# Modulation rows loaded a step ahead, four subtractions moved to VectorE, and a later end for the last group

## The chip, the cores and the metric

The program runs on one core of a Trainium2 chip. Its time is the device time of one execution in microseconds (us). The core has a matrix engine (TensorE, PE in the profile), three engines for elementwise work (VectorE: DVE; ScalarE: ACT; GpSimd: POOL), and a queue on SyncE (SP) that issues nearly all the transfers between HBM and SBUF. Each engine, and the SP queue, takes its instructions strictly in program order; semaphores hold an instruction back until what it reads is there and what it overwrites has been read. Matrix products accumulate in PSUM, which is used as eight banks of 128x512 float32.

## What is computed

The reference is a stack of two layers on one sequence of 1024 tokens with 1024 features in float32. Layer 0 mixes tokens by a forgetting attention (16 heads), layer 1 by a gated linear attention (4 heads, chunks of 64). Each layer is followed by a SwiGLU network of 2816 hidden features. Every part takes an RMS norm that is scaled and shifted by a modulation computed from one conditioning vector, and its output is gated by it:

```python
    c_act = jax.nn.silu(c)
    for i in range(DEPTH):
        mod = c_act @ ada_w[i] + ada_b[i]
        sh1, sc1, g1, sh2, sc2, g2 = jnp.split(mod, N_MOD, axis=-1)
        h = modulate(rms_norm(x, norm1_g[i]), sh1, sc1)
        j = i // N_MIXERS
        if i % N_MIXERS == 0:
            y = forgetting_attention(h, fox_w_in[j], fox_b_f[j], fox_w_out[j])
        else:
            y = gated_linear_attention(h, gla_w_in[j], gla_w_a2[j], gla_b_a[j], gla_g_o[j], gla_w_out[j])
        x = x + g1[:, None, :] * y
        h = modulate(rms_norm(x, norm2_g[i]), sh2, sc2)
        x = x + g2[:, None, :] * swiglu(h, ffn_w_in[i], ffn_w_out[i])
    return rms_norm(x, final_g)
```

`modulate(h, shift, scale)` is `h * (1 + scale) + shift`. `ada_w` is 2 x 1024 x 6144, 48 MB, all of which is read: a modulation is a product of one vector with a 1024x1024 block for each layer and each of the six j.

## The kernel before

**Products.** Every matrix product is done in three passes (`mm3`, L237 to L239): both operands are split in a high and a low part (ACT makes the high part by a cast, L159, DVE the low part by a subtraction, L160), and high x high, low x high and high x low are summed in one PSUM bank. One pass is a matmul of 128x128 with 128x512. So each weight tile costs a load on SP, a cast on ACT, a subtraction on DVE and, where tiles are combined, additions on POOL (L672, L674, L684) before PE may use it.

**Stages.** FoX attention up to about 523 us of the profiled span, its output product and the first network FFN0 up to 1364, the GLA mixer and its output product up to 1817, the second network FFN1 up to the end. Both networks are the same function, `ffn`, on the two layers. It has five stretches:

1. the norm and the operands. Each matrix of h is cut in 2x2 blocks B11, B12, B21, B22 (features by tokens), and sums of blocks T1 to T4 are made as in Winograd's form of Strassen's product, which needs seven block products instead of eight. `second_half` (L1164) makes y12, y22 from x and the norm row, then the raw differences: T1 = y12-y11 on POOL (L1170), y12 = y22-y12 on POOL (L1172, T3 later), y22 = y22-y11 on DVE (L1173, T2), y21 = y21-y22 on POOL (L1176, T4 later). `split_t` splits each in a high part on ACT (L1132, L1135) and a low part on DVE (L1133, L1136).
2. plain tiles (`plain_tile`): a first pair of hidden tiles as ordinary products of 24 matmuls, 672 to 740 us in FFN0. In the trace their weights are called o_s and their banks p_b. At its end the T3 and T4 tiles are split, and `mid()` is called.
3. groups: hidden tiles in groups of seven products of 12 matmuls each (`prod`). ACT applies the Silu, DVE adds products (L1275, into views ex_s of slots "ex"), POOL multiplies gate and up half (L1261) and makes the hidden blocks' sums. 740 to 1100 us in FFN0.
4. output products in seven-product form, summed on DVE (L1447, L1449). In the last round the four groups i = 0..3 of two output rows each are put together: five additions on POOL (L1461 to L1465) and four gates on DVE (L1467, x + g2 * y).
5. the last chunk (`last_chunk`): eight ordinary tiles of 12 matmuls per half of the tokens, f0e01800p_b to f0e01870p_b (f1e... in FFN1), whose result DVE adds to x (L1029). Their banks are a ring pj of three.

**The modulation of layer 1.** The six vectors of layer 1 are computed beside other work. `ada_steps` (L336) is a generator; each step loads a 128-row piece of `ada_w` (L342, SP), multiplies it by a column of c_act (L346, L348, ACT), adds it to an accumulator (L349, POOL), and after eight steps PE sums over the partitions (L365, matmuls mp_b). `ada1` is a `Pace`: each product in the groups calls `ada1(0.64 * n)`, and the yields ADA_A and ADA_B are what a step costs in that currency. `mid0` queues j = 0 and 1 at FFN0's stretch 3 in pieces of 256 columns with an accumulator and **one** raw buffer, both in a view of "ex" (named ex_s); the mixer of layer 1 queues the other four in 512 columns with an accumulator and two raw buffers (named ad_s).

**What sets the order.** A list scheduler orders the whole program: it takes the instructions of the generators as written, models their durations and the semaphores, and puts each engine's instructions in the order in which its model could start them. The order on an engine is then fixed. In FFN0 it draws the modulation's steps ahead of where `mid0` stands: the first ones lie in the tail of the attention's output product, at 613.8 us.

The functions that the change touches, as they are before:

## Time and profile before

| what | us |
|---|---|
| median of 3 runs | 2495.55 |
| lowest, highest run | 2491.82, 2496.45 |
| profiled execution | 2496.43 |
| its span, first to last instruction | 2494.7 |
| PE busy in the span | 2405.8 (96%) |
| DVE, ACT, POOL busy | 1707.5, 1200.8, 1189.9 |

The profile is one execution with a time stamp for every instruction. The views used below are: the groups of instructions by line or by tile with their minimum, median and maximum duration in ns; the list of waits (an instruction, what released it, total us, times, longest); windows (a stretch of the span, the busy time of each engine in it with the count of instructions, the clock that TensorE was granted as a share of full speed, the share of time that DMA engines were busy, GB/s); and the timeline (start, duration, engine, line, instruction; in brackets the idle time ahead of it and what ended that). In the timeline instructions that follow one another on one line are put together in one row with their count and their time together. Names lose their buffer numbers: p_b is any bank of the networks' products, o_s any split weight tile.

### The profile page before, as it was taken

The page shows a single profiled execution, that of the slowest core. Times are in us where ns is not written, and L with a number is a line of the kernel's source. Part 1 is how long each engine was busy: PE and PEld are TensorE (multiplying, and loading weights), DVE is VectorE, ACT ScalarE, POOL GpSimd, SP SyncE. Part 2 cuts the span into 40 slices and gives each one's busy share as a digit, 9 for nine tenths or more (in the row PEclk, how much of TensorE's full clock was granted, in tenths as well). Part 3 has the DMA queues.
Part 4 walks back from the last instruction along what each step waited for, and adds up shares of the span by engine and source line. Part 5 has one row for each costly group of instructions (what it writes and reads, how often), then busy time and mean ns, then how long its engine had stood idle before and what let it go on. Part 6 is the DMA issues. An engine that isn't in the chain of part 4 may idle for free.

```text
span 2494.7 us, 35705 instructions
## 1 busy us (share of the span) xinstructions
PE 2405.8 (96%) x12458; PEld 2040.0 (82%) x12458; DVE 1707.5 (68%) x2829; ACT 1200.8 (48%) x2313; POOL 1189.9 (48%) x1060
## 2 busy tenths in 40 slices
PE   6999999999999989999999999999999999999998
PEld 5888888888878877778887888888878888888887
DVE  6577777676697666675788455445587667666787
ACT  4666565666444443444324665554344333345325
POOL 4233333332466766663354544443345666653263
PEclk9999999999999999999999999999999999999999
DMA  8223333232434544347664333325325434347653
GB/s 263 79 89 115 102 94 119 69 117 93 156 110 159 168 137 160 127 154 266 227 216 156 96 108 99 98 98 174 100 70 188 146 136 152 127 171 261 236 194 131
DMA packets 322813, 359.20 MB, mean 144 GB/s; under 512 B 18557, under 2 KB 255257, under 8 KB 322633
## 3 DMA queue, kind: packets, MB, share of 16 engines
q1 hardware_dynamic: 322632, 356.92, 42.8%
q8 instruction: 98, 1.61, 0.3%
q14 instruction: 83, 0.67, 0.1%
HBM read 268.19 MB, written 88.67 MB: 143 GB/s over the span
## 4 chain that ended last, share of the span: by engine, by line
PE 68%; DVE 10%; DMA 7%; POOL 6%; issue 4%; ACT 3%; SPq 1%; POOLq 0%; DVEq 0%; ACTq 0%
PE p_b L239 11%; PE p_b L237 11%; PE p_b L238 11%; DMA ex_s<-in_ada_w_dram 3%; PE t_b L922 2%; PE o_b L936 2%; PE qk_b L237 2%; PE qk_b L238 2%; PE qk_b L239 2%; DVE o_s L160 1%; DMA ad_s<-in_ada_w_dram 1%; DMA xv_s<-in_ffn_w_out_dram 1%; POOL ex_s L349 1%; PE s_b L891 1%; PE s_b L892 1%
## 5 line engine op out<-in xcount | busy, mean ns | idle before, releaser
L160 DVE TENSOR_TENSOR o_s<-xv_s,o_s 128x512 fp32r<-128x512 f32 (+1 forms) x376 | 328.7, 878 | 117.7 <-ACT o_s L159 117.2
L159 ACT CAST o_s<-xv_s 128x512 fp32r<-128x512 f32 (+1 forms) x376 | 216.2, 585 | 267.7 <-PE p_b L239 222.4
L237 PE MATMUL p_b<-B,o_s 128*128 128x512 f32 x608 | 239.8, 397 | 9.9 <-DVE ex_s L1275 8.1
L239 PE MATMUL p_b<-B,o_s 128*128 128x512 f32 x608 | 240.1, 396 | 8.2 <-DVE o_s L160 8.2
L238 PE MATMUL p_b<-B,o_s 128*128 128x512 f32 x608 | 239.8, 394 | 0.0
L902 POOL TENSOR_SCALAR lp_s<-lp_s,st 128x128 f32<-128x128 f32 (+7 forms) x128 | 95.9, 754 | 293.8 <-DVE st L901 260.7
L672 POOL TENSOR_TENSOR ex_s<-xv_s,xv_s 128x512 f32<-128x512 f32 (+1 forms) x64 | 86.8, 1357 | 254.7 <-DMA xv_s<-in_ffn_w_in_dram 90.7
L237 PE MATMUL p_b<-T,o_s 128*128 128x512 f32 x480 | 188.4, 393 | 6.0 <-ACT o_s L159 4.0
L238 PE MATMUL p_b<-T,o_s 128*128 128x512 f32 x480 | 186.9, 389 | 0.0
L239 PE MATMUL p_b<-T,o_s 128*128 128x512 f32 x480 | 183.5, 390 | 0.7 <-DVE o_s L160 0.7
L237 PEld LDWEIGHTS p_b<-B,o_s 128*128 128x128 f32 x608 | 116.0, 191 | 37.3 <-DVE ex_s L1275 9.8
L239 PEld LDWEIGHTS p_b<-B,o_s 128*128 128x128 f32 x608 | 116.0, 191 | 33.6 <-DVE o_s L160 9.0
L238 PEld LDWEIGHTS p_b<-B,o_s 128*128 128x128 f32 x608 | 116.1, 191 | 24.6 <-DVE B L1136 0.6
L900 ACT ACTIVATE lp_s<-lp_s,st 128x128 f32<-128x128 f32 (+7 forms) x128 | 99.3, 776 | 55.9 <-DVE st L896 55.3
L159 ACT CAST pt_s<-t_b 128x512 fp32r<-128x512 f32 (+1 forms) x160 | 80.1, 547 | 71.2 <-PE t_b L922 70.3
L1275 DVE TENSOR_TENSOR ex_s<-ex_s,p_b 128x512 f32<-128x512 f32 x140 | 93.5, 679 | 27.8 <-PE p_b L239 27.8
L237 PEld LDWEIGHTS p_b<-T,o_s 128*128 128x128 f32 x480 | 90.1, 188 | 27.4 <-ACT o_s L159 6.2
L160 DVE TENSOR_TENSOR pt_s<-t_b,pt_s 128x512 fp32r<-128x512 f32 (+1 forms) x160 | 96.5, 630 | 17.7 <-ACT pt_s L159 17.1
L239 PEld LDWEIGHTS p_b<-T,o_s 128*128 128x128 f32 x480 | 90.1, 188 | 21.4 <-DVE o_s L160 2.5
L238 PEld LDWEIGHTS p_b<-T,o_s 128*128 128x128 f32 x480 | 90.2, 188 | 18.3
L205 POOL TENSOR_TENSOR w_l_s<-w__s,w_h_s 128x256 fp32r<-128x256 f32 x90 | 69.6, 801 | 68.1 <-ACT w_h_s L202 58.6
L896 DVE CUSTOM_DVE_ANT_0 lp_s<-s_b,cum_s 128x512 f32<-128x512 f32 (+3 forms) x128 | 72.6, 569 | 40.5 <-PE t_b L922 22.9
(1941 smaller groups left out, 7636.2 us busy)
## 6 DMA issues: line engine op xcount, KB each, us to landing
xv_s<-in_ffn_w_in_dram SPq DMA_DIRECT2D x176, 256.0 KB, 3.0
hid_B<-x SPq DMA_DIRECT2D x70, 512.0 KB, 2.6
hid_T<-x SPq DMA_DIRECT2D x36, 512.0 KB, 2.7
xv_s<-in_ffn_w_out_dram SPq DMA_DIRECT2D x96, 192.0 KB, 4.4
ada_s<-in_ada_w_dram SPq DMA_DIRECT2D x32, 512.0 KB, 3.8
ad_s<-in_ada_w_dram SPq DMA_DIRECT2D x64, 256.0 KB, 2.7
xv_s<-in_ffn_w_out_dram SPq DMA_DIRECT2D x40, 256.0 KB, 3.0
T1o<-hid_T SPq DMA_DIRECT2D x18, 512.0 KB, 8.3
```

The lines of the kernel that those rows point to most:

```text
L159: nc.scalar.copy(hi, src)
L160: nc.vector.tensor_sub(lo, src, hi.bitcast(F32))
L205: (nc.gpsimd if i < 3 else nc.vector).tensor_sub(lo[:, cs], rw[:, cs], hi[:, cs].bitcast(F32))
L237: nc.tensor.matmul(ps, ah, bh, start=start, stop=False)
L238: nc.tensor.matmul(ps, ah, bl, start=False, stop=False)
L239: nc.tensor.matmul(ps, al, bh, start=False, stop=stop)
L672: nc.gpsimd.tensor_add(s1, a21, a22)
L896: nc.vector.tensor_tensor_reduce(lp[:, k0:k1], ps, cm[:, k0:k1], 1.0, mcur, ALU.add, ALU.min, mnew)
L900: nc.scalar.activation(lp, lp, AF.Exp, bias=mcur, scale=-1.0, accum_out=st[:, qi, 2:3])
L902: nc.gpsimd.tensor_scalar(lp, lp, st[:, qi, 3:4], 1.0, op0=ALU.mult, op1=ALU.mult)
L922: nc.tensor.transpose(tp[:, i, :], lps[qi][:, psl(2 * b + jj)], ident)
L1275: nc.vector.tensor_add(d, d if src is None else dest(G, src), ps)
```

## The change

Line numbers of the changed kernel are 11 to 30 higher: L342, L348, L349 become L345, L360, L361; L1029, L1461 to L1467 become L1040, L1478 to L1482.

1. **Modulation.** `ada_steps` issues the load of a step before it works on the step ahead of it (`got` holds one loaded piece in advance). In FFN0 the pieces have 512 columns instead of 256, and lie in views of slots "hid" with three raw buffers instead of one; these views are also ya, so they are free only when T2 and T4 are split. 64 loads of 128 KB become 32 of 256 KB, and the 64 multiplications and 56 additions become 32 and 28 of twice the width. The steps' costs are 6.0 and 3.0 instead of 5.0 and 2.5, and `ada1` is emptied before the group before the last, ahead of the tiles that take "hid" again.
2. **T3, T4.** The subtractions of T3 and T4 are done on DVE, and in the program they stand where T3 and T4 are split, behind the plain tiles. So that y22 and y12 last until then, T2's difference is written over y11 instead.
3. **Last group.** The five additions of the last group are done on DVE and are put, one or two at a time with the gates, behind the first outputs of the last chunk (`meanwhile`). The ring pj of the last chunk has six banks instead of three in layer 0 and four instead of three in layer 1.

```diff
--- before.py
+++ after.py
@@ -335,12 +335,24 @@
 
     def ada_steps(l, j, acc_of, raw_of, w):
 
+        steps = deque((c0, k) for c0 in range(0, D, w) for k in range(8))
+        got = deque()
+
+        def load():
+            if steps:
+                c0, k = steps.popleft()
+                raw = raw_of([P, w], F32, f"ada{l}{j}{c0}{k}")
+                nc.sync.dma_start(raw, ada_w[l, psl(k), j * D + c0:j * D + c0 + w])
+                got.append(raw)
+
         for c0 in range(0, D, w):
             acc = acc_of([P, w], F32, f"acc{l}{j}{c0}")
             for k in range(8):
-                raw = raw_of([P, w], F32, f"ada{l}{j}{c0}{k}")
-                nc.sync.dma_start(raw, ada_w[l, psl(k), j * D + c0:j * D + c0 + w])
+                if w == D or c0 == k == 0:
+                    load()
+                raw = got.popleft()
                 if w < D:
+                    load()
                     yield ADA_A
                     if k == 0:
                         nc.scalar.mul(acc, raw, cact[:, 0:1])
@@ -487,7 +499,6 @@
 
     sp_ins, rb_ins = [], []
     LATE1 = 7
-    TE = (nc.gpsimd, nc.gpsimd, nc.vector, nc.gpsimd)
     GK = (2, 6)
     SPM, RBM = (3, 4)
 
@@ -1031,7 +1042,7 @@
                 if after is not None:
                     after(m, hf)
 
-    def last_chunk(k0, kc, hs, xs, l, j, nm, v, norm, mt=2, each=None):
+    def last_chunk(k0, kc, hs, xs, l, j, nm, v, norm, mt=2, each=None, meanwhile=None):
 
 
         behind = None
@@ -1042,6 +1053,8 @@
                 sq(m, xs[m][:, hsl(h_)])
                 if each:
                     each(m, h_)
+                if meanwhile:
+                    meanwhile()
             run(out_chunk(k0, kc, hs, xs, l, j, f"{nm}{hf}", (hf,), after,
                           mt=mt, behind=behind))
             behind = norm(hf, sq.roots)
@@ -1167,13 +1180,10 @@
                 normed(y22[k], k + 4, 1, rb)
                 split_t(B22[k], y22[k], sh(k + 4))
             for k in range(4):
-                TE[0].tensor_sub(y11[k], y12[k], y11[k])
+                nc.gpsimd.tensor_sub(y11[k], y12[k], y11[k])
                 split_t(T1[k], y11[k])
-                TE[1].tensor_sub(y12[k], y22[k], y12[k])
-                TE[2].tensor_sub(y22[k], y22[k], y11[k])
-                split_t(T2[k], y22[k], sh(k + 4))
-            for k in range(4):
-                TE[3].tensor_sub(y21[k], y21[k], y22[k])
+                nc.vector.tensor_sub(y11[k], y22[k], y11[k])
+                split_t(T2[k], y11[k], sh(k + 4))
 
         x_sp = tc.dram_tile([8, P, S], F32, name=f"x_sp{l}")
         for k in range(8):
@@ -1312,10 +1322,12 @@
         block("T3", H_SL[4:8])
         T3 = b["T3"]
         for k in range(4):
+            nc.vector.tensor_sub(y12[k], y22[k], y12[k])
             split_t(T3[k], y12[k], ds[:, k:k + 1])
         block("T4", slots["to"])
         T4 = b["T4"]
         for k in range(4):
+            nc.vector.tensor_sub(y21[k], y21[k], y11[k])
             split_t(T4[k], y21[k])
         mid()
         bk = list(pin.q)
@@ -1361,7 +1373,7 @@
                     load_raw(ahead)
                 yield
 
-        hp, xr, zs = {}, {}, {}
+        hp, xr, zs, ends = {}, {}, {}, deque()
 
         def last_part():
 
@@ -1392,6 +1404,7 @@
         for X in gs[2:]:
             up = lambda n: advance(n) if X is gs[-1] else None
             if X is gs[-2]:
+                ada1.flush()
                 nxt[0] = part(0)
                 advance(4)
             nc.scalar.copy(dest(X, C11), prod(feed.next(), B11))
@@ -1457,22 +1470,39 @@
                 onto(Y1, p_(4))
                 onto(Y2, p_(5))
                 onto(Y3, p_(6), False)
-                if last:
-                    nc.gpsimd.tensor_add(Y1, Y1, Z1)
-                    nc.gpsimd.tensor_add(Y4, Y4, Z1)
-                    nc.gpsimd.tensor_sub(Y2, Y4, Y2)
-                    nc.gpsimd.tensor_add(Y4, Y4, Z5)
-                    nc.gpsimd.tensor_sub(Y3, Y4, Y3)
-                    for (a, hf), v_ in (((0, 0), Y1), ((1, 0), Y2), ((1, 1), Y4), ((0, 1), Y3)):
-                        nc.vector.scalar_tensor_tensor(v_, v_, mcol(l, 5, 2 * i + a), xr[(a, hf)],
-                                                       op0=ALU.mult, op1=ALU.add)
+                if not last:
+                    continue
+                V = nc.vector if i == 3 else nc.gpsimd
+
+                def gated(a, hf, v_, i=i):
+                    nc.vector.scalar_tensor_tensor(v_, v_, mcol(l, 5, 2 * i + a), xr[(a, hf)],
+                                                   op0=ALU.mult, op1=ALU.add)
+                fins = [lambda: V.tensor_add(Y1, Y1, Z1), lambda: V.tensor_add(Y4, Y4, Z1),
+                        lambda: V.tensor_sub(Y2, Y4, Y2), lambda: V.tensor_add(Y4, Y4, Z5),
+                        lambda: V.tensor_sub(Y3, Y4, Y3)]
+                gates_ = [lambda a=a, hf=hf, v_=v_: gated(a, hf, v_)
+                          for (a, hf), v_ in (((0, 0), Y1), ((1, 0), Y2), ((1, 1), Y4), ((0, 1), Y3))]
+                if i < 3:
+                    for f in fins + gates_:
+                        f()
+                else:
+                    ends.extend([fins[0], gates_[0], fins[1], fins[2], gates_[1], None, fins[3], None, fins[4], None,
+                                 gates_[2], None, gates_[3]])
         ada1.flush()
         bk = sorted(bk)
-        pin, pj = Ring(psp, bk[:5]), Ring(psp, bk[5:])
+        n = 4 if each else 2
+        pin, pj = Ring(psp, bk[3:3 + n]), Ring(psp, bk[:3] + bk[3 + n:])
+
+        def meanwhile():
+
+            for _ in range(2):
+                f = ends.popleft() if ends else None
+                if f:
+                    f()
         sv = Views(slots["b"][0:4], 2, [HALF], f"se{l}").v
         tmp = Views(slots["to"], 2, [HALF], f"te{l}")
         last_chunk(NFH - 4, 4, hp, xs, l, 5, f"f{l}e", sv,
-                   lambda hf, ss: norm_end(hf, ss, tmp), mt=1, each=each)
+                   lambda hf, ss: norm_end(hf, ss, tmp), mt=1, each=each, meanwhile=meanwhile)
 
     pin = None
     slots = ffn_slots(rest)
@@ -1484,10 +1514,10 @@
         return norm_half(xs, ss, hs1, 1, hf, Ring(psp, ["b3", "b4"]), tmp)
 
     def mid0():
-        v = opr_["ada"]
-        ada1_queue((0, 1), v[:, 0:256], [v[:, 256:512]], 256)
-
-    ADA_A, ADA_B = 5.0, 2.5
+        v = Views(slots["hid"], 2, [HALF], "ad0").v
+        ada1_queue((0, 1), v[0], v[1:4], HALF)
+
+    ADA_A, ADA_B = 6.0, 3.0
     ffn(0, oh, xs, slots, "fo", mid0, norm_mixer)
     h1 = hs1
     dump("xb0", xs)
```

Where the scheduler puts it, at three places. The first is the SP queue in FFN0's groups. Before (L342 the modulation's loads, L654 the weights', L1208 the hidden blocks' stores):

```order
L1208 DMA hid_T_7509<-sg_s_7648 128x512
L1208 DMA hid_T_7507<-x_4_6128 128x1024
L654 DMA xv_s_7331<-in_ffn_w_in_dram 128x4x128
L342 DMA ex_s_7330<-in_ada_w_dram 128x256
L654 DMA xv_s_7331<-in_ffn_w_in_dram 128x4x128
L342 DMA ex_s_7330<-in_ada_w_dram 128x256
L654 DMA xv_s_7332<-in_ffn_w_in_dram 128x4x128
L342 DMA ex_s_7330<-in_ada_w_dram 128x256 x2
L654 DMA xv_s_7332<-in_ffn_w_in_dram 128x4x128
L342 DMA ex_s_7330<-in_ada_w_dram 128x256 x2
```

And now, L345 the modulation's loads, L665 the weights', L1218 the stores:

```order
L345 DMA ad_s_7847<-in_ada_w_dram 128x512
L665 DMA xv_s_7332<-in_ffn_w_in_dram 128x4x128 x2
L345 DMA ad_s_7847<-in_ada_w_dram 128x512
L345 DMA ad_s_7846<-in_ada_w_dram 128x512
L665 DMA xv_s_7333<-in_ffn_w_in_dram 128x4x128
L345 DMA ad_s_7847<-in_ada_w_dram 128x512 x2
L665 DMA xv_s_7333<-in_ffn_w_in_dram 128x4x128
L345 DMA ad_s_7846<-in_ada_w_dram 128x512
L1218 DMA hid_B_7475<-x_4_6128 128x1024
L665 DMA xv_s_7331<-in_ffn_w_in_dram 128x4x128 x2
```

Eight steps lie close together in both, four times instead of eight, and the first of them now lies behind the plain tiles and not in the attention's tail. In the mixer of layer 1 the 64 loads of ad_s and ACT's multiplications stand in the same order before and now.

The second place is DVE at the end of FFN0's plain tiles. T_7444 to T_7447 are T2's tiles, o_s_8 the weights' low part that PE waits for there. Before:

```order
L1173 TENSOR_TENSOR yb_s_7450<-yb_s_7450,ya_s_7035 128x512 x2
L1133 TENSOR_TENSOR x_2_6126<-sg_s_7616,x_2_6126 128x512
L1173 TENSOR_TENSOR yb_s_7451<-yb_s_7451,ya_s_7036 128x512 x2
L160 TENSOR_TENSOR o_s_7_7763<-xv_s_7331,o_s_7_7763 128x512
L160 TENSOR_TENSOR o_s_9_7846<-xv_s_7332,o_s_9_7846 128x512
L1136 SCALAR_TENSOR_TENSOR T_7444<-yb_s_7450,modc,T_7444 128x512
L1136 SCALAR_TENSOR_TENSOR T_7445<-yb_s_7450,modc,T_7445 128x512
L1136 SCALAR_TENSOR_TENSOR T_7446<-yb_s_7451,modc,T_7446 128x512
L1136 SCALAR_TENSOR_TENSOR T_7447<-yb_s_7451,modc,T_7447 128x512
L160 TENSOR_TENSOR o_s_8_7778<-xv_s_7331,o_s_8_7778 128x512
```

And now (L1325 makes T3's difference, L1185 T2's, L1330 T4's):

```order
L1146 TENSOR_TENSOR x_2_6126<-sg_s_7608,x_2_6126 128x512
L160 TENSOR_TENSOR o_s_7_7755<-xv_s_7331,o_s_7_7755 128x512
L160 TENSOR_TENSOR o_s_9_7850<-xv_s_7332,o_s_9_7850 128x512
L1330 TENSOR_TENSOR ya_s_7037<-ya_s_7037,ya_s_7035 128x512
L1185 TENSOR_TENSOR ya_s_7036<-yb_s_7451,ya_s_7036 128x512
L1149 SCALAR_TENSOR_TENSOR T_7444<-ya_s_7035,modc,T_7444 128x512
L1330 TENSOR_TENSOR ya_s_7037<-ya_s_7037,ya_s_7035 128x512
L1330 TENSOR_TENSOR ya_s_7038<-ya_s_7038,ya_s_7036 128x512
L1149 SCALAR_TENSOR_TENSOR T_7445<-ya_s_7035,modc,T_7445 128x512
L1149 SCALAR_TENSOR_TENSOR T_7446<-ya_s_7036,modc,T_7446 128x512
L160 TENSOR_TENSOR o_s_8_7770<-xv_s_7331,o_s_8_7770 128x512
```

All four of T3's subtractions and three of T4's stand ahead of o_s_8, although the program has them behind the plain tiles; one of T2's splits has gone behind it. On POOL the rows of L1172 and L1176 are gone.

The third place is DVE at the first tiles of FFN0's last chunk (L1029 takes a bank out, L1467 gates, L704 splits weights). Before:

```order
L1467 SCALAR_TENSOR_TENSOR x_6_6130<-x_6_6130,modc,ex_s_7328 128x512
L704 TENSOR_TENSOR oo_s_237_12497<-xv_s_7332,oo_s_237_12497 128x512
L1449 TENSOR_TENSOR x_6_6130<-x_6_6130,p_b_84_12429 128x512
L1467 SCALAR_TENSOR_TENSOR x_7_6131<-x_7_6131,modc,ex_s_7329 128x512
L704 TENSOR_TENSOR oo_s_238_12516<-xv_s_7332,oo_s_238_12516 128x512
L1029 SCALAR_TENSOR_TENSOR x_0_6124<-f0e01800p_b_1_12461,modc,x_0_6124 128x512
```

And now (L1478, L1480 to L1482 are the moved additions and the gates, L1040 takes a bank out):

```order
L1478 SCALAR_TENSOR_TENSOR x_6_6130<-x_6_6130,modc,ex_s_7328 128x512
L715 TENSOR_TENSOR oo_s_237_12394<-xv_s_7332,oo_s_237_12394 128x512
L1481 TENSOR_TENSOR x_7_6131<-x_7_6131 128x512
L1462 TENSOR_TENSOR x_6_6130<-x_6_6130,p_b_84_12331 128x512
L715 TENSOR_TENSOR oo_s_238_12416<-xv_s_7332,oo_s_238_12416 128x512
L1478 SCALAR_TENSOR_TENSOR x_7_6131<-x_7_6131,modc,ex_s_7329 128x512
L1481 TENSOR_TENSOR x_7_6131<-x_7_6131,z_10895 128x512
L1040 SCALAR_TENSOR_TENSOR x_0_6124<-f0e01800p_b_1_12354,modc,x_0_6124 128x512
```

The first bank is still taken out behind two gates, with two of the additions between them; the last gates now stand between the first banks' rows.

## The prediction

> **What bounds the kernel now.** I read the busy times first, then the windows of FFN0 beside FFN1, then the waits, then the timelines of PE's gaps.
>
> ```profile
> PE 2405.8 (96%) x12458; PEld 2040.0 (82%) x12458; DVE 1707.5 (68%) x2829; ACT 1200.8 (48%) x2313; POOL 1189.9 (48%) x1060
> ```
>
> PE sets the time: only what lets it idle, or run at a lower clock, can be won. The two networks issue the same products, and only FFN0 carries the modulation, so FFN1 is the measure of FFN0. Of the tile p_b alone:
>
> ```profile
> 759.75:856.17 96.42, 96.02 (x421) 78.62 (x420) 22.84 (x34) 2.88 (x5) 1.00 0.52 174
> 1906.17:2001.38 95.21, 95.21 (x422) 78.83 (x421) 23.38 (x35) 2.88 (x5) 1.00 0.46 157
> 856.17:1074.62 218.45, 200.66 (x842) 157.97 (x840) 46.45 (x70) 5.72 (x10) 0.98 0.43 145
> 2001.38:2191.78 190.40, 190.40 (x842) 157.66 (x841) 46.78 (x70) 5.75 (x10) 1.00 0.40 140
> ```
>
> The same 842 matmuls take 218.45 us in FFN0 and 190.40 in FFN1 (0.2261 a matmul, no idle time): 28.1 lost, and 1.2 more in the stretch ahead: **29.3 us**. What FFN0 waits for there:
>
> ```profile
> ACT ex_s L348 <- DMA ex_s<-in_ada_w_dram: 107.6, 53, 5.7
> ACT ad_s L348 <- DMA ad_s<-in_ada_w_dram: 39.0, 30, 3.8
> SPq L342 <- POOL ex_s L349: 110.1, 50, 4.6
> PE p_b L237 <- DVE ex_s L1275: 8.7, 5, 2.1
> ```
>
> With one raw buffer a step is a closed chain: load, ACT, POOL, next load. ACT stands 107.6 us before a load, with the casts of the weights queued behind it; SP stands 110.1 us before a load that waits for POOL, with the weights' loads behind it. PE shows the end of it: about 2 us a burst, through L1275, which waits for a view that POOL is late to release. In the mixer, with two buffers, the wait is 39.0 us for as many steps.
>
> **The change part by part: the modulation.**
>
> ```profile
> L348 ACT ACTIVATE ex_s<-ex_s,cact x56: 493/510/513, 619.5 to 1060.0; 128x256 f32<-128x256 f32 x56
> L349 POOL TENSOR_TENSOR ex_s<-ex_s x56: 723/737/1266, 620.1 to 1060.7; 128x256 f32<-128x256 f32 x56
> L365 PEld LDWEIGHTS mp_b<-ones,ex_s x32: 187/190/192, 756.3 to 1071.6; 128*128 128x128 f32 x32
> L348 ACT ACTIVATE ad_s<-ad_s,cact x56: 706/724/734, 1376.8 to 1691.8; 128x512 f32<-128x512 f32 x56
> L349 POOL TENSOR_TENSOR ad_s<-ad_s,ad_s x32: 1256/1300/1834, 1378.8 to 1692.9; 128x512 f32<-128x512 f32 x32
> DMA to landing us min/median/max: 2.6/2.7/5.6
> ```
>
> Work: ACT from 64 x 0.51 = 32.6 to 32 x 0.72 = 23.0 us; POOL from 56 x 0.74 = 41.4 to 28 x 1.30 = 36.4; 32 fewer issues on SP. PE's 32 matmuls mp_b stay, at most 32 x 0.19 = 6.1 us. So 29.3 - 6.1 = 23 us can surely be got back, 29.3 at most if those matmuls cost nothing. Whether they are got back rests on the new bursts. With three buffers a load waits for the addition three steps back, and 2.7 us of load lie beside other steps. POOL:
>
> ```profile
> 856.17:1074.62 218.45, 201.80 (x862) 160.64 (x860) 140.01 (x174) 89.27 (x167) 146.94 (x117) 0.98 0.43 145
> 2001.38:2191.78 190.40, 190.40 (x842) 157.66 (x841) 133.11 (x166) 73.65 (x126) 121.11 (x81) 1.00 0.40 140
> ```
>
> (all engines: PE, weight loads, DVE, ACT, POOL). Without the modulation POOL is busy 121.11 of 190.40, 64%. In the new order the eight loads of a burst lie across some 131, 81, 80 and 62 matmuls, 29.6, 18.3, 18.1 and 14.0 us at 0.2261. Their additions (7 x 1.30 = 9.1) and 64% come to 27.9, 20.7, 20.6 and 18.0: POOL falls behind by 0, 2.4, 2.5 and 4.0 us, 8.9 in all, with over 30 us of products behind each but the last, a third of them free on POOL, and with five weight tiles in hand (`depth` 5; 5 x 12 x 0.2261 = 13.6 us). The cover is that lead; without it 8.9 us come back. I take **22**, between 0 (the chain stays) and 29.
>
> The first burst also leaves the attention's tail:
>
> ```profile
> 645.30:661.32 16.02, 14.53 (x65) 11.76 (x65) 11.16 (x16) 7.45 (x14) 10.93 (x11) 0.89 0.69 217
> 1793.90:1806.62 12.72, 12.72 (x67) 10.75 (x65) 8.30 (x12) 5.45 (x10) 5.31 (x5) 1.00 0.69 229
> 649.33 0.51 ACT L348 ACTIVATE ex_s<-ex_s,cact 128x256 f32<-128x256 f32 x1 [3.02 <-DMA ex_s<-in_ada_w_dram]
> ```
>
> The same matmuls take 16.02 us here and 12.72 behind the mixer: 3.3 lost, where ACT waits 3.02 for a modulation load ahead of the squares and casts. I take **2.5** (0 to 3.3).
>
> In the mixer the loads and multiplications keep their order, so its 39.0 us of waits stay and so does its time: **0**. Emptying `ada1` ahead of the group before the last costs nothing, since in the new order the last addition lies ahead of it. The bytes are the same, and DMA engines are busy 0.43 of the groups' time.
>
> **T3 and T4.** The same thing happens in both layers:
>
> ```profile
> 691.82 3.60 DVE L1136 SCALAR_TENSOR_TENSOR B<-yb_s,modc,B 128x512 fp32r<-128x512 f32 x3
> 699.35 2.43 DVE L1136 SCALAR_TENSOR_TENSOR B<-yb_s,modc,B 128x512 fp32r<-128x512 f32 x2
> 705.59 9.76 POOL L1176 TENSOR_TENSOR ya_s<-ya_s,yb_s 128x512 f32<-128x512 f32 x4 [5.02 <-DVE yb_s L1173]
> 695.35 1.78 DVE L1133 TENSOR_TENSOR T<-ya_s,T 128x512 fp32r<-128x512 f32 x1
> 698.75 0.68 DVE L1133 TENSOR_TENSOR T<-ya_s,T 128x512 fp32r<-128x512 f32 x1
> 709.05 6.84 DVE L1136 SCALAR_TENSOR_TENSOR T<-yb_s,modc,T 128x512 fp32r<-128x512 f32 x4
> 715.82 1.74 DVE L160 TENSOR_TENSOR o_s<-xv_s,o_s 128x512 fp32r<-128x512 f32 x1
> 717.61 0.50 PE L239 MATMUL p_b<-B,o_s 128*128 128x512 f32 x1 [4.09 <-DVE o_s L160]
> 695.90:720.50 24.60, 20.51 (x85) 16.28 (x84) 24.60 (x28) 10.41 (x19) 15.40 (x8) 0.96 0.13 44
> 720.50:740.20 19.70, 19.70 (x85) 16.23 (x84) 19.70 (x22) 8.27 (x16) 12.67 (x8) 0.97 0.55 195
> 1842.77:1867.39 24.62, 20.53 (x85) 16.31 (x85) 24.62 (x27) 10.39 (x19) 15.44 (x8) 0.96 0.13 44
> ```
>
> DVE is full (24.60 of 24.60), and beside POOL's subtractions its instructions are longer: a split 1.78 us beside POOL, 0.68 without; four of T 6.84, which at about 0.7 would be 2.8. PE stands 4.09 us until the low part o_s is done at 717.56. Loss per layer 24.60 + 19.70 - 170 x 0.2261 = 5.9 us. After: with POOL's subtractions the lengthening ahead of o_s goes: 6.84 - 2.8 = 4.0, 1.74 - 0.68 = 1.1, and earlier, beside L1172, 3.60 - 2.1 = 1.5, 1.78 - 0.68 = 1.1 and 2.43 - 1.4 = 1.0, together 8.7. Seven subtractions come ahead of it, each some 0.6 (a split without POOL is 0.68 and overlaps its neighbour): 4.3; one split of T goes behind it, 0.7. So o_s ends near 717.6 - 8.7 + 4.3 - 0.7 = 712.5, and PE needs it at 717.61 - 4.09 = 713.5: a microsecond to spare. What is late next is T4's split, for which the groups leave time: its first use is the sixth product of the first group. Gain 5.0 of 5.9 a layer, **10** for two (0, if all stays as long as now, to 11.8).
>
> The Trainium skill's "SBUF — State Buffer", section "Who interferes with whom", says that a VectorE instruction with two SBUF inputs contends with a GpSimd instruction that reads SBUF, and that issue order decides who blocks. The rows at 695.35 and 698.75 agree. The rule speaks against the change, since the moved subtractions have two SBUF inputs too; by it each of 13 on DVE could grow by 1.1 us wherever POOL still works, and the gains here and at the last chunk would be gone (the second rival).
>
> **The last group.**
>
> ```profile
> 1313.30 1.74 POOL L1461 TENSOR_TENSOR x<-x,z 128x512 f32<-128x512 f32 x1
> 1315.08 1.76 DVE L1467 SCALAR_TENSOR_TENSOR x<-x,modc,ex_s 128x512 f32<-128x512 f32 x1 [0.59 <-POOL x L1461]
> 1316.76 1.77 DVE L704 TENSOR_TENSOR oo_s<-xv_s,oo_s 128x512 fp32r<-128x512 f32 x1
> 1321.38 0.74 DVE L1029 SCALAR_TENSOR_TENSOR x<-f0e01800p_b,modc,x 128x512 f32<-128x512 f32 x1
> 1322.27 0.47 PE L237 MATMUL f0e01830p_b<-hh,oo_s 128*128 128x512 f32 x1 [4.49 <-DVE x L1029]
> 1309.46:1337.59 28.13, 23.64 (x98) 19.11 (x96) 23.92 (x31) 9.19 (x15) 10.46 (x7) 0.94 0.41 122
> 2426.52:2456.98 30.46, 26.12 (x109) 21.09 (x108) 25.21 (x33) 13.92 (x24) 10.49 (x7) 0.89 0.41 122
> 2438.45 0.74 DVE L1029 SCALAR_TENSOR_TENSOR x<-f1e01800p_b,modc,x 128x512 f32<-128x512 f32 x1
> ```
>
> The fourth tile needs the first of three banks, which L1029 empties at 1321.38, behind lengthened splits. Lost: 28.13 - 96 x 0.2261 = 6.4 us, and 30.46 - 109 x 0.2261 = 5.8 in FFN1. With six banks the seventh tile is the first that needs one, 6 x 2.71 = 16.3 us from 1309.5, at 1325.7: no wait even at today's pace. With four the fifth tile needs it at 2426.5 + 10.9 = 2437.4; L1029 ends at 2439.2 now, less three splits and gates that are longer by about 1.05 each, as above, and 0.6 of idle, plus four additions ahead of it at 0.61: 2437.9, half a microsecond late. The transposes at the very end have four banks in place of five, which I cost at nothing, since four still keep three free beside the one that PE fills. I take **10** (0 to 12.2).
>
> **Sum**: 22 + 2.5 + 10 + 10 = 44.5 us. Span 2494.7 - 44.5 = 2450.2, that execution 2496.4 - 44.5 = 2451.9, and the median of the runs, 0.9 us under that execution, **2451**.
>
> **The rivals.**
>
> 1. *The bursts cost.* POOL's 8.9 us come through to PE, with a stretch at lower clock behind each gap. After a 2.09 us gap at 1016 the granted clock was:
>
> ```profile
> 1020.00:1030.00 10.00, 10.00 (x42) 8.16 (x42) 8.17 (x9) 3.02 (x6) 8.47 (x6) 0.89 0.44 159
> ```
>
> That is 10 x 0.11 = 1.1 us each time. 8.9 + 4 x 1.1 less the 1 to 3 allowed for: 10 to 12 us, **2462**. For it: denser bursts; against: the lead. ("TensorE: Matmul & The Clock Gate", section "What's actually happening", in the Trainium skill, has half rate after an idle window of about 3.4 us; this row shows it behind a gap of 2.09, so it disagrees. By that rule this rival would be 2458.)
>
> 2. *DVE stays late.* The moved subtractions are lengthened in their turn, by the weight combinations that POOL starts earlier (L674 now waits behind L1176). T3/T4 and the last group bring 10 instead of 20: **2461**. For it: DVE is full there. Against: 20 us of lengthening come from the very instructions that go, and the six banks need nothing of DVE.
>
> 3. *The chain returns, slower than before.* The bursts are as dense in loads as POOL is in additions; if each of SP's loads waits for POOL, POOL for a weight behind that load, a step costs 2.7 + 0.72 + 1.30 and one 1.3 of POOL's other work, 6.0 us. Eight take 48 us against some 20 us of products in a burst and 13.6 of lead: 14.4 us late, four times 58. In place of the 22 us that the forecast takes off, 58 - 23 = 35 come on: 2451 + 22 + 35, **2508**. It decides above 4.2 us a step, (20 + 13.6) / 8, and the kernel is slower than before above some 5.6. For it: the 110.1 us on SP. Against: the mixer's same width with two buffers.
>
> 4. *The modulation brings nothing*: its views come free with T4, late, and hold SP, so that all of it moves without a gain; only 2.5 + 20 us remain: **2473**.
>
> **How the numbers follow.** Forecast 0.55 (its own range 2443 to 2458), rivals one and two 0.15 each, the third 0.08, the fourth 0.07. Under 2441 nothing is left to win (29 + 3.3 + 11.8 + 12.2 = 56 at most, 2439). The range 2441 to 2474 takes in the first two rivals and just reaches the fourth. A measurement of this kernel tells a change from none above about 0.2%, 5 us. Only the third rival is not faster: slower 0.05, the same 0.03, faster 0.92.
>
> **What would show it.** Right: FFN0's 842 matmuls between 190 and 200 us; no wait of PE for o_s L160 of 4 us; no gap ahead of f0e01830p_b and f1e01810p_b, at most 1 us at the fifth tile of FFN1; the attention's tail at 13 to 14 us; unchanged ACT waits of about 39 us in the mixer. Wrong: ACT or SP waits for the modulation in FFN0 of more than 50 us, gaps of PE inside the four bursts, T's splits still at 1.7 us, or a mixer that became shorter or longer by over 2 us.

## The result, and the profile after

| | before | changed |
|---|---|---|
| median of 4 runs, us | 2495.94 | 2453.88 |
| lowest, highest run | 2491.82, 2496.45 | 2447.10, 2458.51 |
| span of the profiled execution | 2494.7 | 2454.1 |

The time is 0.9833 of before (95% interval 0.9806 to 0.9859), 42 us less. Forecast were 2451 us and a range of 2441 to 2474. In the changed kernel's page PE is busy for 98% instead of 96%:

```profile
PE 2393.3 (98%) x12458; PEld 2038.0 (83%) x12458; DVE 1697.8 (69%) x2849; ACT 1193.6 (49%) x2281; POOL 1153.2 (47%) x1006
```

PE issues the same 12458 instructions in both kernels, so the two spans can be cut at the same matmuls. Each row below is the time between two such starts, in the two profiled executions:

| stretch | before | changed | difference |
|---|---|---|---|
| start to the attention's output tail | 648.06 | 649.93 | +1.9 |
| attention's tail, fo1411 to fo1441 | 13.26 | 9.92 | -3.3 |
| FFN0: first 192 matmuls of the plain tiles | 54.29 | 49.65 | -4.6 |
| FFN0: matmul 192 to 300, into the groups | 24.48 | 28.89 | +4.4 |
| FFN0: matmul 300 to 756 | 105.09 | 105.39 | +0.3 |
| FFN0: matmul 756 to 1596 | 218.45 | 195.15 | -23.3 |
| FFN0: first seven tiles of the last chunk | 25.41 | 19.16 | -6.3 |
| from there to the mixer's output tail | 461.83 | 462.62 | +0.8 |
| FFN1: first 192 matmuls of the plain tiles | 55.92 | 51.24 | -4.7 |
| FFN1: matmul 192 to 2520 | 527.67 | 527.69 | 0.0 |
| FFN1: first seven tiles of the last chunk | 26.72 | 19.16 | -7.6 |
| the rest, norms and the end of FFN1 among it | | | +1.7 |

The sum is -40.7 us, the difference of the two spans. The tile p_b alone in FFN0, in the view that showed 218.45 before:

```profile
720.50:749.40 28.90, 25.07 (x110) 20.12 (x108) 5.41 (x8) 1.14 (x2) 1.00 0.69 234
749.40:854.78 105.38, 104.58 (x457) 85.32 (x456) 25.20 (x38) 2.86 (x5) 1.00 0.55 179
854.78:1049.94 195.16, 191.85 (x842) 157.31 (x841) 47.19 (x71) 5.74 (x10) 1.00 0.44 152
```

The third row has come within 5 us of FFN1's 190.40. The first has grown: there PE idles 1.06 and 2.77 us at 737 and 745 us. The waits between 600 and 1150 us (L360 is the multiplication, L345 the load):

```profile
ACT ad_s L360 <- DMA ad_s<-in_ada_w_dram: 32.7, 21, 5.0
SPq L345 <- POOL ad_s L361: 26.0, 20, 2.4
```

ACT stood 107.6 us and SP 110.1 us there before. The plain tiles, DVE's timeline (L1149 splits T2, L160 is the low part that PE waited for), and below it the 192 matmuls in FFN0 and FFN1:

```profile
707.96 1.79 DVE L1149 SCALAR_TENSOR_TENSOR T<-ya_s,modc,T 128x512 fp32r<-128x512 f32 x1
709.67 1.28 DVE L1330 TENSOR_TENSOR ya_s<-ya_s,ya_s 128x512 f32<-128x512 f32 x2
710.87 1.40 DVE L1149 SCALAR_TENSOR_TENSOR T<-ya_s,modc,T 128x512 fp32r<-128x512 f32 x2
712.20 0.68 DVE L160 TENSOR_TENSOR o_s<-xv_s,o_s 128x512 fp32r<-128x512 f32 x1
```

```profile
670.85:720.50 49.65, 45.90 (x192) 36.99 (x192) 1.35 (x2) 2.38 (x4) 0.97 0.26 85
1788.01:1839.25 51.24, 46.78 (x193) 37.49 (x192) 1.35 (x2) 2.38 (x4) 0.93 0.18 62
```

One of T2's splits is still 1.79 us long, beside a weight combination on POOL; the others are 0.70 and the moved subtractions 0.64. o_s is done at 712.88, and the wait of 4.09 us is gone. The last chunk's first seven tiles, with all engines:

```profile
1285.31:1304.47 19.16, 19.16 (x85) 15.84 (x85) 18.35 (x30) 6.69 (x12) 3.63 (x2) 1.00 0.48 140
2392.64:2411.80 19.16, 19.16 (x84) 15.84 (x85) 18.44 (x30) 8.85 (x16) 3.63 (x2) 1.00 0.47 139
```

PE is busy for 19.16 of 19.16 us in both layers; DVE is still nearly full.

### The profile page after: what moved, and what is told of

It is laid out like the page before. It is cut to its first block, busy times and chain, and to the rows that moved or that the text cites. A ratio compares the mean times of both kernels' runs of the same rounds, so it can differ in the third digit from the quotient of the medians.

```text
span 2454.1 us, 35528 instructions
## 1 busy us (share of the span) xinstructions
PE 2393.3 (98%) x12458; PEld 2038.0 (83%) x12458; DVE 1697.8 (69%) x2849; ACT 1193.6 (49%) x2281; POOL 1153.2 (47%) x1006
## 4 chain that ended last, share of the span: by engine, by line
PE 79%; DVE 8%; DMA 4%; ACT 3%; POOL 3%; issue 2%; SPq 0%; DVEq 0%; POOLq 0%; ACTq 0%
PE p_b L237 14%; PE p_b L239 14%; PE p_b L238 14%; PE o_b L947 2%; PE t_b L933 2%; PE qk_b L237 2%; PE qk_b L238 2%; PE qk_b L239 2%; DMA ad_s<-in_ada_w_dram 2%; POOL ad_s L361 1%; PE s_b L902 1%; PE s_b L903 1%; PE vps_b L237 1%; PE vps_b L239 1%; PE vps_b L238 1%
## 5 line engine op out<-in xcount | busy, mean ns | idle before, releaser
L160 DVE TENSOR_TENSOR o_s<-xv_s,o_s 128x512 fp32r<-128x512 f32 (+1 forms) x376 | 326.4, 872 | 87.5 <-ACT o_s L159 87.0
L159 ACT CAST o_s<-xv_s 128x512 fp32r<-128x512 f32 (+1 forms) x376 | 217.4, 587 | 304.4 <-PE p_b L239 261.2
L1285 DVE TENSOR_TENSOR ex_s<-ex_s,p_b 128x512 f32<-128x512 f32 x140 | 94.0, 681 | 36.5 <-PE p_b L239 36.3
L159 ACT CAST pt_s<-t_b 128x512 fp32r<-128x512 f32 (+1 forms) x160 | 80.1, 547 | 71.0 <-PE t_b L933 69.8
L685 POOL TENSOR_TENSOR xv_s<-ex_s,xv_s 128x512 f32<-128x512 f32 (+1 forms) x64 | 84.4, 1318 | 61.0 <-DVE o_s L160 58.8
L160 DVE TENSOR_TENSOR pt_s<-t_b,pt_s 128x512 fp32r<-128x512 f32 (+1 forms) x160 | 96.6, 631 | 17.7 <-ACT pt_s L159 17.0
```

The costliest lines, as they stand in the source:

```text
L159: nc.scalar.copy(hi, src)
L160: nc.vector.tensor_sub(lo, src, hi.bitcast(F32))
L685: nc.gpsimd.tensor_sub(a11, s1, a11)
L1285: nc.vector.tensor_add(d, d if src is None else dest(G, src), ps)
```

## The experiments

All comparisons of stretches are cut at the same matmuls. The **loss in the groups** below is the time of FFN0 from matmul 192 to 1596 less 318.24 us, which FFN1 takes for it. Line numbers differ by a few from kernel to kernel.

### One part at a time

The modulation alone (parts 2 and 3 of the change left as before), T3/T4 alone, the last group alone; and the whole change with the first burst later. The edits in this section are shortened. The kernel before was run again beside each set of experiments, with medians of 2497.07, 2492.65 and 2494.85 us, so kernels of different sets are compared by the share of before and not by their medians.

```diff
 e4_later, against the changed kernel
+        hold = None
+        if l == 1 and j == 0:
+            yield 18.0
+            hold = (the last instruction on SP so far)
...
+                    if hold is not None and c0 == 0:
+                        es.enter_context(tc.issue_after(hold))
                     nc.sync.dma_start(raw, ada_w[...])
```

> Before with the modulation's part alone (512 columns, three raw buffers in the views of hid, emptied ahead of the group before the last); T3, T4 and the last group as before. In the changed kernel the 842 matmuls take 195.15 us instead of 218.45, the attention's tail 9.92 instead of 13.26, and 4.9 us are newly lost where the plain tiles end and the groups begin (gaps of 1.06 and 2.77 us at 737 and 745). Theory 'burst': these 4.9 us belong to the modulation's first burst, which comes when the weights' lead is not yet built. Then they are here too: 2495.9 - 23.3 - 3.3 + 4.4 = about 2474. Theory 'late T4': they belong to T3 and T4's later subtractions on VectorE. Then the border of plain tiles and groups is as before (24.5 us from matmul 192 to 300) and the time is about 2469.

> Before with T3's and T4's subtractions on VectorE alone. Both layers' plain tiles (first 192 matmuls) should be 4.6 us shorter, the wait for o_s of 4.09 us gone in both: 2495.9 - 9.3 = about 2486.6. Theory 'burst': the next 108 matmuls stay at 24.5 us. Theory 'late T4': they take some 29 us in FFN0, and 2491.

> Before with the last group's additions on VectorE behind the last chunk's first outputs and six or four banks, alone. From the changed kernel's trace: 6.3 us in FFN0, 7.6 less about 1 behind it in FFN1: 2495.9 - 13 = about 2483. If the parts lean on each other (the last chunk was shorter only because other parts freed POOL), less: 2488 or more.

> The changed kernel with the modulation's first load queued on SyncE behind the weights of the twelfth product of the groups, so that all four bursts move one group (84 matmuls) later; nothing else. Theory 'burst without lead': the gaps of 1.06 and 2.77 us at the start of the groups go with the slow stretch behind them, and no gap of this size comes in their place: 2453.9 - 4.9 = about 2449. Rival 'a burst costs the same anywhere': the gaps come back one group later and the time stays at 2454.

| | median, us | of before (95% interval) |
|---|---|---|
| modulation alone | 2474.34 | 0.9909 (0.9892 to 0.9925) |
| T3/T4 alone | 2482.32 | 0.9939 (0.9924 to 0.9953) |
| last group alone | 2482.22 | 0.9939 (0.9919 to 0.9959) |
| all, first burst later | 2456.18 | 0.9837 (0.9821 to 0.9853) |

The border of plain tiles and groups, tile p_b, with the modulation alone, then with T3/T4 alone (and its plain tiles in both layers):

```profile
724.33:755.72 31.39, 26.85 (x110) 21.05 (x109) 5.34 (x8) 1.15 (x2) 0.95 0.62 203
```

```profile
720.75:745.23 24.48, 24.48 (x109) 20.27 (x108) 5.33 (x8) 1.15 (x2) 1.00 0.68 223
671.10:720.75 49.65, 45.62 (x192) 36.56 (x192) 1.35 (x2) 2.37 (x4) 0.97 0.19 64
1809.35:1859.01 49.66, 45.67 (x192) 36.88 (x192) 1.36 (x2) 2.38 (x4) 0.97 0.19 64
```

The loss at the border belongs to the modulation's first burst, as the theory 'burst' had it: 31.39 with the modulation alone, and nothing (24.48) with T3/T4 alone, which has its own gain in full. T3/T4's median fell by 14.8 us, more than the 9.3 that I had expected. Its plain tiles give 4.6 and 6.3 us and its groups 2.1; 1.6 of the second is the clock (last section). The last group alone has 19.13 and 19.16 us for the seven tiles, as in the whole change, so the parts do not lean on each other there. The three falls of the medians, 22.7, 14.8 and 14.9 us, add up to 52, ten more than the whole change brings. By the profiled executions they are 20.5, 14.9 and 8.3, against 40.7. So one median is good to a few us only (the four runs of the last group alone lie between 2478.04 and 2488.12), and the price of a part is better read from its stretches.

The chain that makes the gap at 745 us can be read from the changed kernel's timeline (L361 modulation add, L695 weight combination, L360 multiplication, L159 and L160 weights' split, L1285 takes a bank out):

```profile
743.29 1.29 POOL L361 TENSOR_TENSOR ad_s<-ad_s,ad_s 128x512 f32<-128x512 f32 x1
745.21 1.26 POOL L695 TENSOR_TENSOR xv_s<-xv_s,xv_s 128x512 f32<-128x512 f32 x1 [0.63 <-DVE o_s L160]
740.85 0.72 ACT L360 ACTIVATE ad_s<-ad_s,cact 128x512 f32<-128x512 f32 x1 [1.76 <-DMA ad_s<-in_ada_w_dram]
742.83 1.13 ACT L159 CAST o_s<-xv_s 128x512 fp32r<-128x512 f32 x2
743.47 1.66 DVE L160 TENSOR_TENSOR o_s<-xv_s,o_s 128x512 fp32r<-128x512 f32 x1 [1.46 <-ACT o_s L159]
745.65 1.37 DVE L160 TENSOR_TENSOR o_s<-xv_s,o_s 128x512 fp32r<-128x512 f32 x1
746.94 0.67 DVE L1285 TENSOR_TENSOR x<-x,p_b 128x512 f32<-128x512 f32 x1
747.67 0.50 PE L237 MATMUL p_b<-B,o_s 128*128 128x512 f32 x1 [2.77 <-DVE x L1285]
```

The weights' casts stand on ACT behind a multiplication that has waited 1.76 us for its load; DVE's low part waits 1.46 us for the first of them; DVE's addition at 746.94, which frees a bank, stands behind two low parts; PE waits for the bank. The queues pass a late load on from engine to engine. But the late load is not all of it: the two low parts take 1.66 and 1.37 us instead of 0.68, beside the modulation's addition at 743.29 and the weight combination at 745.21 on POOL. That is 1.7 us more, as much as the wait, and no run separates the two.

The later burst speaks against my explanation, by which the first burst is dear only because it comes when the weights' lead is not yet built:

```profile
717.46:741.94 24.48, 24.48 (x109) 20.28 (x108) 5.33 (x8) 1.15 (x2) 1.00 0.61 205
741.94:856.77 114.83, 107.61 (x457) 85.94 (x456) 25.53 (x38) 2.86 (x5) 0.99 0.54 176
856.77:1051.10 194.33, 191.85 (x842) 157.27 (x840) 46.91 (x70) 5.74 (x10) 1.00 0.47 160
```

The border is clean, but the next stretch takes 114.83 instead of 105.38. The loss in the groups is 15.4 us against 11.2. The rival holds: the burst costs no less one group later. The lead itself was not measured.

### Width, buffers and place

```diff
 e5_one_buffer, against the changed kernel (and the load back in the step itself)
-        ada1_queue((0, 1), v[0], v[1:4], HALF)
+        ada1_queue((0, 1), v[0], v[1:2], HALF)
 e6_256
+        ada1_queue((0, 1), v[0][:, 0:256], [v_[:, 0:256] for v_ in v[1:4]], 256)
 e10_old_later (and the load back in the step itself)
+        ada1_queue((0, 1), v[0][:, 0:256], [v[1][:, 0:256]], 256)
 e11_none
-        ada1_queue((0, 1), v[0], v[1:4], HALF)
+        nc.vector.memset(modc[:, 1, 0:2, :], 0.0)
+        make_a(1, 0)
```

The last leaves out layer 1's first two modulation vectors.

> The changed kernel, its modulation in FFN0 still in 512 columns and at the same place, but with one raw buffer instead of three (and so each load behind the addition of the step before). Theory 'buffers': the closed chain of load, ACT, POOL costs PE time, however many steps it has. With 32 instead of 64 steps of 2.7 + 0.72 + 1.30 us the loss in the groups (29.3 us before, about 11 now) comes back in part, to some 15 to 22: 2458 to 2465. Rival 'width': the gain comes from half as many steps and the place behind the plain tiles alone, and the buffers do nothing: 2454.

> The changed kernel with three raw buffers in the same views, but 256 columns instead of 512 (64 steps in eight bursts, costs 5.0 and 2.5). Theory 'buffers': most of the gain is kept, with 5 us more of POOL and 10 us more of ACT: 2453 to 2459, and shorter bursts could make the gaps smaller. Rival 'width': the steps' number decides, and about half of the 18.6 us of the groups is lost: 2463 or more.

> The changed kernel with the modulation of FFN0 as before (256 columns, one raw buffer, load in the step itself, costs 5.0 and 2.5), only in the views of hid and so behind the plain tiles. Loss of PE in FFN0 from matmul 192 to 1596 against FFN1: 29.8 us before, 11.2 in the change, 16.1 with one buffer of 512 columns, 13.7 with three of 256. Theory 'steps of the closed chain': 64 steps of a chain with one buffer cost about 29 wherever they stand: 2472. Rival 'place': the gain came from moving the work behind the plain tiles, and the loss is 11 to 16: 2454 to 2459.

> The changed kernel without the modulation's two vectors in FFN0 (j = 0, 1 of layer 1 are set to zero; 32 loads, 32 multiplications, 28 additions and 32 small matmuls are left out), all else the same. It measures what the modulation still costs. If the 11.2 us still lost in FFN0's groups are all its own, FFN0 takes there what FFN1 takes (318.2 us from matmul 192 to 1596), and the time is 2453.9 - 11.2 = about 2443. If T3/T4's later split has a part in the gaps at 737 and 745 us, 3 to 4 us stay there: 2446.

Tile p_b from matmul 192 to 1596, one buffer of 512 columns; three of 256; one of 256; without the modulation; and, last, FFN1 of the kernel before, which all are measured by:

```profile
719.27:1053.61 334.34, 324.82 (x1406) 261.82 (x1404) 77.85 (x116) 9.75 (x17) 1.00 0.50 167
```

```profile
719.96:1051.91 331.95, 323.70 (x1405) 263.62 (x1404) 77.43 (x116) 9.74 (x17) 0.99 0.50 168
```

```profile
715.12:1062.45 347.33, 328.46 (x1405) 262.38 (x1404) 76.56 (x115) 9.74 (x17) 1.00 0.48 159
```

```profile
718.72:1036.96 318.24, 318.24 (x1406) 263.51 (x1404) 77.63 (x116) 9.78 (x17) 1.00 0.44 150
```

```profile
1873.54:2191.78 318.24, 318.24 (x1406) 263.52 (x1405) 77.64 (x116) 9.79 (x17) 1.00 0.43 150
```

| loss in the groups, us (PE's idle time in it; ACT's wait for loads there) | one raw buffer | three |
|---|---|---|
| 256 columns | 29.1 (17.1; 105.4) | 13.7 (5.8; 53.2) |
| 512 columns | 16.1 (7.9; 58.2) | 11.2 (6.3; 32.7) |

Each cell is one execution. How far two of them can be told apart is shown by the kernels with the banks alone and with the additions alone (last experiment), which run the same groups as the changed kernel in the same order: their losses are 12.9 and 12.7 us, with 6.4 us of idle time. In each of them the granted clock fell to half for 3.41 us at one gap, and in the changed kernel's groups it did not. All engines in the kernel with the banks alone, behind its gap of 2.54 us, then in the changed kernel around the same gap, 2.48 us there:

```profile
865.72:869.13 3.41, 3.41 (x10) 2.67 (x9) 3.09 (x4) 1.19 (x3) 2.64 (x3) 0.50 0.70 207
864.00:880.00 16.00, 13.52 (x63) 10.96 (x62) 12.42 (x16) 6.41 (x11) 8.37 (x7) 1.00 0.49 160
```

Medians: 2455.52 (0.9854, 0.9839 to 0.9868) with one buffer of 512 columns, 2454.87 (0.9849, 0.9835 to 0.9864) with three of 256, 2471.40 (0.9903, 0.9888 to 0.9918) with one of 256, 2441.94 (0.9788, 0.9773 to 0.9802) without the modulation.

- **Place** is worth nothing in the groups: the old scheme behind the plain tiles loses 29.1 us, 29.8 where it was. (Its 3.3 us in the attention's tail it does give back.)
- **Width or buffers**, either alone, bring 13.0 and 15.4 us; both together 17.9, or 16.2 as the kernel with the banks alone has it, and not 28. Whether three buffers of 512 columns lose less than three of 256 is not shown: the idle time is no smaller (6.3 against 5.8), and of the 2.5 us between the losses some 1.6 are the price of such a slow stretch, which the kernel with three of 256 has once in its groups. Half as many turns of a closed chain, or an open one, are two remedies for one wait, and ACT's wait for loads falls with both.
- **Loading ahead** brings nothing by itself. With the load put back into the step and all else as changed, the scheduler writes the same program, row for row on every engine: it had drawn each load as far forward as the buffers allowed.
- **All that is still lost there is the modulation's**: without it FFN0 takes 318.24 us, FFN1's time to the hundredth. T3/T4 have no part in it.

Of the 11.2 us that remain, the gaps of 1.06, 2.77 and 2.48 us are 6.3, the 32 small matmuls take 2.9 (the sum of the distances from their starts to the next start), and 2.0 are slower matmuls: 0.8 at the gaps, 0.8 right behind the small matmuls, the rest in small pieces.

### Can the rest be spread, or moved to VectorE?

Both edits are shortened; `e12_dve` concerns j = 0 and 1 of layer 1 alone, and its first step of eight is a multiplication without the accumulator.

```diff
 e9_paced, against the changed kernel
+                    if l == 1 and j < 2:
+                        es.enter_context(tc.issue_after(the last instruction on SP so far))
                     nc.sync.dma_start(raw, ada_w[...])
 e12_dve
-                        nc.scalar.mul(raw, raw, cact[:, k:k + 1])
-                        nc.gpsimd.tensor_add(acc, acc, raw)
+                        nc.vector.scalar_tensor_tensor(acc, raw, cact[:, k:k + 1], acc, op0=ALU.mult, op1=ALU.add)
```

> The changed kernel with every load of the modulation in FFN0 queued on SyncE behind the last load that the program had issued by then, so that its 32 steps are spread over the groups (about one in three and a half products) instead of four bursts of eight. Theory 'bursts': what is still lost in the groups beyond PE's own 32 small matmuls (4.4 us at their start, 2.48 us and the like later) comes from POOL and ACT being full for 15 to 30 us; spread out, the gaps above 1 us go: 2447 to 2450. Rival 'each step costs': the loss belongs to the work, not to its density, and stays about 11 us: 2454.

> The changed kernel with each modulation step of FFN0 as one instruction on VectorE (raw x c + accumulator) in place of a multiplication on ACT and an addition on POOL. Theory 'POOL late': what is still idle in the groups (6.3 us, gaps at 737, 745 and 865) comes from POOL's additions and ACT's waits for loads; VectorE is busy 70% there and takes 32 x about 0.74 = 24 us more, over 318: gaps gone, 2446 to 2449. Rival 'VectorE is the late engine': its instructions wait for the loads in its queue, ahead of the splits that PE needs, and the gaps grow: 2460 or more.

Paced 2449.13 us (0.9828, 0.9811 to 0.9844), on VectorE 2452.72 (0.9834, 0.9819 to 0.9848): neither can be told from the change's 0.9833. The stretch, paced and on VectorE:

```profile
716.01:1046.91 330.90, 322.51 (x1406) 263.96 (x1404) 76.80 (x115) 9.76 (x17) 0.99 0.50 168
```

```profile
717.82:1051.74 333.92, 324.39 (x1405) 264.93 (x1404) 78.15 (x116) 9.86 (x17) 0.99 0.49 166
```

Losses of 12.7 and 15.7 us; the first can't be told from the 11.2 to 12.9 of the bursts. Spread out, two gaps of 1.86 and 1.17 us stay in the products, but PE now waits where the sum over the partitions stands, and its idle time is 6.2 us against 6.3; with VectorE it waits for a bank behind the steps in DVE's queue:

```profile
947.40 0.61 PE L381 MATMUL mp_b<-ones,ad_s 128*128 128x1 f32 x4 [2.23 <-POOL ad_s L365]
```

```profile
885.86 1.77 DVE L360 SCALAR_TENSOR_TENSOR ad_s<-ad_s,cact,ad_s 128x512 f32<-128x512 f32 x1
890.92 0.74 DVE L360 SCALAR_TENSOR_TENSOR ad_s<-ad_s,cact 128x512 f32<-128x512 f32 x1
894.07 0.47 PE L237 MATMUL p_b<-B,o_s 128*128 128x512 f32 x1 [4.54 <-DVE x L1289]
```

Bursts are therefore not shown to be the cause of the rest. With more columns or more buffers the loss stayed at 11 to 16 us wherever the steps went; whether another order hides it is open. The low median of the paced kernel is not explained by its groups, and I don't count it as a gain: the kernel before ran 3.3 us lower beside it, too, than in the result.

### Banks or additions

```diff
 e7_banks: additions as before (POOL, at the group's end), but
+        n = 4 if each else 2
+        pin, pj = Ring(psp, bk[3:3 + n]), Ring(psp, bk[:3] + bk[3 + n:])
 e8_moved: additions as changed, but
+        pin, pj = Ring(psp, bk[:5]), Ring(psp, bk[5:])
```

> The changed kernel with the five additions of the last group on POOL ahead of the last chunk, as before, but the six and four banks of the change. Theory 'banks': in FFN0 the first bank to be reused is needed 16.3 us after the first tile, so its gap of 4.49 us is gone with the banks alone; in FFN1 the fifth tile needs a bank at 10.9 us, which is emptied at about 12.7: a gap of about 2 us stays. f0e01800 to f0e01870 takes 19.2 to 19.6 us, f1e 21 to 23: 2456 to 2458. Rival 'additions': the bank comes late because VectorE's work is long beside POOL, and both gaps stay in large part: 2463.

> The changed kernel with three banks in the last chunk, as before, but the additions moved to VectorE as in the change. Theory 'banks decide': the fourth tile of FFN0 needs its bank 8.1 us after the first tile's start, and VectorE, rid of POOL, empties it at about 10.8 us (five additions and gates ahead of it): a gap of 2 to 3 us with a slow stretch stays in each layer; f0e01800 to f0e01870 takes 22 to 24 us instead of 19.16: 2459 to 2462. Rival 'additions decide': both at 19.2 to 20 us: 2454 to 2455.

Seven tiles, FFN0 and FFN1, banks only (with PE's one gap), then additions only (with the gaps of both):

```profile
1282.92:1302.08 19.16, 19.16 (x84) 15.85 (x85) 18.57 (x23) 5.45 (x10) 9.52 (x7) 1.00 0.40 121
2387.43:2408.13 20.70, 19.40 (x85) 15.76 (x85) 18.76 (x24) 8.57 (x16) 10.53 (x7) 1.00 0.42 123
2399.85 0.47 PE L237 MATMUL f1e01840p_b<-hh,oo_s 128*128 128x512 f32 x1 [1.30 <-DVE x L1041]
```

```profile
1282.50:1304.86 22.36, 19.32 (x85) 15.69 (x84) 21.43 (x34) 7.70 (x13) 3.64 (x2) 1.00 0.43 130
2393.99:2418.41 24.42, 21.72 (x93) 17.57 (x92) 21.13 (x34) 11.15 (x20) 2.64 (x2) 0.93 0.41 122
1288.42 0.47 PE L237 MATMUL f0e01810p_b<-hh,oo_s 128*128 128x512 f32 x1 [3.04 <-DVE x L1462]
2402.28 0.50 PE L237 MATMUL f1e01810p_b<-hh,oo_s 128*128 128x512 f32 x1 [2.70 <-DVE x L1462]
```

Before, the change: 25.41 and 26.72, then 19.16 and 19.16. The banks alone bring 6.3 and 6.0 us, in FFN0 the whole of it; in FFN1, with four banks, the fifth tile waits 1.30 us (some 2 were expected), which only the moved additions take away. The additions alone bring 3.1 and 2.3 against before. With the modulation alone, which leaves the last group as it was, the same tiles take 23.82 and 25.27 us, so as much as 1.6 and 1.4 of that need not be the additions'. Medians 2455.48 (0.9858, 0.9842 to 0.9875) and 2460.01 (0.9851, 0.9833 to 0.9869).

The edit of the banks does more than add some. The sorted list of banks has eight; before, the ring had the last three, and now its first three tiles take the first three of the list (`bk[:3]`). This matters in FFN1, where PE's wait before the change was not at the fourth tile for the ring's first bank, as in FFN0, but at f1e01810, for a bank that still held a product of the groups (L1449 takes it out):

```profile
2435.51 0.68 DVE L1449 TENSOR_TENSOR x<-x,p_b 128x512 f32<-128x512 f32 x1
2436.24 0.79 PE L237 MATMUL f1e01810p_b<-hh,oo_s 128*128 128x512 f32 x1 [4.34 <-DVE x L1449]
```

The kernel with the additions alone has the old banks and waits at f0e01810 and f1e01810 (3.04 and 2.70 us, L1462 being the former L1449). So in FFN0 the wait moved from the fourth tile to the second, and the expectation, 2 to 3 us at the fourth tile, came out in size but not in place. That the bank is late behind lengthened instructions of DVE fits in both layers: in FFN1 two of 1.73 and 1.74 us, at 2432.18 and 2433.84, stand ahead of the row at 2435.51. Whether FFN1 needed more banks or only banks that were emptied earlier, no run separates.

## Why the prediction was right

Point by point, with the prediction's sum of 44.5 us beside what the two traces show.

| term | forecast | measured | held or not |
|---|---|---|---|
| modulation, groups of FFN0 | 22 | 18.6 | mechanism held, size too large |
| modulation, attention's tail | 2.5 | 3.3 | held: the whole loss |
| mixer of layer 1 | 0 | within 0.8 | held: same order, same time |
| T3/T4, both layers | 10 | 9.3 | held |
| last group, both layers | 10 | 13.8 | held in FFN0; in FFN1 another wait; too small |
| sum | 44.5 | 45.0 | |

The two spans differ by 40.7. The 4.3 between lie in other places: 1.9 ahead of the attention's tail, 0.8 from FFN0's last chunk to the mixer's output tail, and 1.7 in the rest, around the networks' norms and at the end. Their causes are open. Ahead of the attention's tail the eleven kernels with the modulation moved do the same work, and their profiled executions differ by up to 3.8 us there.

That the sum is met within half a microsecond is therefore luck in part: the modulation brought 3.4 less than forecast, the last group 3.8 more, and 4.3 us in other places were in no term. That each of the three parts brings time, and where, was not luck: each does so alone.

**The modulation.** The closed chain was the cause of the larger part of the loss, as the two-by-two table shows: fewer turns or more buffers take away 13 to 18 of 29 us. The step of the prediction that was too good is "The cover is that lead; without it 8.9 us come back." The lead of weights did not cover all of it: 6.3 us of gaps came through, with 0.8 of slow restart behind them, and putting the first burst one group later did not help. Gaps of PE inside the bursts were among the signs named for being wrong, and two of the three gaps lie in the first burst. What I left out is that a burst also delays weights through ACT, whose queue holds the casts behind multiplications that wait for loads, that POOL's additions lengthen DVE's splits, and that DVE passes both on to PE's banks. My first rival had this loss, at 10 to 12 us beyond the forecast. Of it 3.4 us came, and the last group made up for them.

PE's own 32 small matmuls, bounded by 6.1 us in the prediction, take 2.9.

**T3 and T4.** o_s was forecast to end near 712.5 and ended at 712.88. The second rival, VectorE late again, did not come about. The Trainium skill's rule on two SBUF inputs ("SBUF — State Buffer", "Who interferes with whom") is seen once more, in the one split of 1.79 us beside POOL; the moved subtractions met POOL idle, and cost 0.6 us each. So the rule, which spoke against the change, holds here and found little to act on.

**The last group.** I had taken 10 of 12.2 because the fifth tile of FFN1 looked half a microsecond late. It was not late. The fourth tile and L1029, on which that term rests, are right for FFN0 alone; in FFN1 PE waited at f1e01810 for L1449, and what took this wait away is that the first tiles now lie in other banks. The sign that I had named, no gap ahead of f1e01810p_b, came true, but the sum does not explain why. And the loss in FFN1 was 7.6 us, not 5.8: the window that I took held 13 matmuls beside the 96 of the tiles, and I charged each at the price of a full one. The expected wait at the fifth tile is there, 1.30 us, only if the additions stay on POOL.

**The third and fourth rival** are refuted: the kernel is 42 us faster, the groups gained 18.6 of them, ACT's and SP's waits in FFN0 fell to 32.7 and 26.0 us, below the 50 named as the mark.
